# One core, a hybrid encoder layer: the side work of an attention block issued between the two score maps of the next block

## The chip, the cores and the metric

The kernel runs on one core of a Trainium2 chip. The metric is the device time of one execution in microseconds (us). The profile names the engines PE (TensorE, matmuls and transposes), PEld (its weight loads, which overlap), DVE (VectorE), ACT (ScalarE), POOL (GpSimd) and SP (SyncE, which issues nearly all DMAs of this kernel, in order); a suffix q stands for an engine's queue of such issues.

## The reference: what is computed

A layer of 1024 positions by 1024 channels in float32: a modulated RMS norm, one input projection, and two groups of four heads each on its result. Group A is a gated linear attention in both directions, computed in 16 chunks of 64 positions (GLA). Group B is a differential attention: two softmax maps for each head, the second subtracted with a factor. Their outputs go side by side through one output projection and are added to the input; a gated MLP with a convolution of width 3 and a last RMS norm follow.

```python
# GLA, one direction: S_t = diag(a_t) S_(t-1) + k_t v_t^T
chunk_update = jnp.einsum('bhnsd,bhnsv->nbhdv', k_st, v)
def step(S, inp):
    upd, dec = inp
    return dec[..., None] * S + upd, S
_, S_prev = lax.scan(step, S0, (chunk_update, chunk_decay))
o_inter = jnp.einsum('bhncd,nbhdv->bhncv', q_in, S_prev)
...
# differential attention, one block of 128 queries
s = jnp.einsum('bhiqd,bhikd->bhiqk', q_blk, k).astype(jnp.float32) * scale
s = s + bias.transpose(0, 3, 1, 2)[:, :, None]
p = jax.nn.softmax(s, axis=-1)
a = p[:, :, 0] - lam * p[:, :, 1]
return jnp.einsum('bhqk,bhkv->bhqv', a, v.astype(jnp.float32))
...
mixed = jnp.concatenate([o_a, o_b], axis=-1) @ w_out[i]
x = x + g_a[:, None, :] * mixed
```

## The kernel before, in words

The program runs through the projection, the attention, the up-projection and the down-projection in this order, with pieces of the next stage drawn into the one before. Up to the projection the instructions stand as written; from the attention on, a scheduler orders each engine's instructions at build time, from a model of when operands are ready, with the order of the program as priority. So a step that is issued earlier in the program moves ahead on every engine on which it stands, though not by a fixed number of rows.

The differential attention runs over 32 blocks of 128 queries: for each half of the positions, heads 0 to 3, four blocks each (`seq`, blocks 0 to 3 of all heads, then 4 to 7). `att_seq` (L1261) goes over them as a software pipeline whose rows are a string of steps, and the digit behind a letter is how many blocks ahead that step works:

```python
for i in range(-3, len(seq) + 3):
    for what, rest in todo:
        at = i + int(rest.rstrip("ab") or 0)
```

- `l` is `att_load` (L827): the queries of two blocks (L832) and the bias of one (L702), all on SP.
- `pa` and `pb` are `att_probs` for the first and the second map: scores on PE (`s`, L842), bias and row minimum on DVE (`p`, `mx`, L845), the exponential on ACT (L850).
- `m` is `att_mix` on DVE: L856, L858, and L860, which joins both maps into one.
- `t` is `att_T`: eight transposes on PE (`aT_ps`, L869), half copied by ACT (L871) and half by DVE (`aT`, L873).
- `o` is `att_out`: eight matmuls on PE (`o`, L888), the scaling on DVE (`on`, L889), and for the last block of a head and half the norm (ACT L895 to L897, POOL L898), whose result the next block transposes (L907) and stores (L921, L922).
- `s` is `side` (L1362), the work that goes along with block `at`. In some blocks it loads the keys of the next head (`load_k`, L817). In the first 16 blocks it takes steps of the GLA heads, in the order that the entry `glas` gives, from 1 to 3 steps a block; in the second 16 it takes steps of the output projection of the first half of the positions (L1288 on: loads L1313 and L1301, matmuls L565 to L567, the sum L1325, the transposes L380).

The GLA steps are four kinds for each head:

```python
'glas': 'L0 S0 L1 C0 S1 O0 L2 C1 S2 O1 L3 C2 S3 O2 C3 O3'
```

- `L` loads its keys, values and queries (L1010 to L1012, `gk`, `gv`, `gq`).
- `S`, the state, works in two groups: four transposes of the keys on PE (`kn_ps`, L1028), their copy on ACT (`kn`, L1029), sixteen matmuls on PE (`u_ps_0`, `u_ps_1`, L1034), copies on ACT into the state (`gs`, L1039, L1041).
- `C`, the scan, is 14 steps on DVE, each on the result of the one before (`gs`, L1049), then four DMAs on SP that rearrange the state (L1055, L1056).
- `O`, the output, works on two halves: masked scores (`pf` and `pb` on PE, L1071 and L1074; both masks on DVE, L1075 and L1076, into one buffer `att` of which there is one in all), the product (`go`, L1082 and L1085), its copy and square on ACT (L1088, `gsq` L1090), the mean on PE (`ms`, L1095), two activations on ACT (L1096, L1097), a product on DVE (L1098), one on POOL (L1099), the split into a high and a low part (ACT cast L370 `ohi`, POOL L371) and two stores on SP (L1103, L1104).

`mm` PSUM banks (two) serve `kn_ps`, `u_ps`, `pf`, `pb`, `go` and `ms`; two `ao` banks serve the transposes and `o`; two banks of double size serve the scores `s`.

Of the kernel before, what the change touches and what calls it, by code (L numbers as in the profile page):

```python
# [76 lines left out]

@with_exitstack
def hymba_kernel(ctx, tc, ins, bounds, out):
    KN = {'seq': 'X2 X3 X0 X1 Z0123 A2 A3 A0 G1 U0 C0 b0av W0v R0 g0 X4 Q1:8 W1v Q1 C1 b1av g1 N0 X5 X6 X7 Z4567 A4 A5 Q2:4 A6 G7 Q2:4 c0av Q2:4 c1av k0 Q2 C2 b2av k1 Q3:8 c2av g2 Q3 C3 b3av k2 c3av T0 P0 g3 k3 M0 E0 F0', 'att': 'l2 p1a p1b m0 t0 s0 o0', 'bias': (0, 3), 'lam': (2, 3), 'behind': (1, 2), 'sy': 7, 'wos': {'qk1': 0.75, 'gr0': 0.75, 'gr1': 0.75}, 'ord': 'gqk1 vd gv qk0 qk1 gr0 gr1 qk2 qk3', 'pf': {'gqk1': 1, 'vd': 2, 'gv': 4, 'qk0': 1, 'qk1': 1, 'qk2': 1, 'gr0': 1, 'qk3': 1, 'gr1': 1}, 'gla': [1, 2, 2, 3, 3, 3, 3, 3, 3, 3, 3, 3, 3, 3, 3, 3], 'w0': 13, 'kd': 2, 'wo': [3, 2, 2, 2, 2, 2, 1, 1, 2, 4, 3, 3, 3, 2, 3, 3], 'i1': 26, 'late': 1, 'x01': (3, 4), 'h2g': 2, 'aT': 0, 'h2y': 4, 'ld': 'x2 x3 p x0 a1 x1 a0 g x4 | r A1 h x5 x6 x7 A2 A3', 'tabs': 0, 'ada': {'gqk1': 0.75, 'vd': 1, 'gv': 1, 'qk0': 1, 'qk1': 1}, 'pre': {'gv': 0.5, 'qk0': 1.25, 'gr0': 1.25, 'qk1': 1.25, 'gr1': 1.25}, 'tab': {'vd': 1, 'gv': 1}, 'early': {'qk3': 1.25}, 'glas': 'L0 S0 L1 C0 S1 O0 L2 C1 S2 O1 L3 C2 S3 O2 C3 O3', 'aq': 1}  # L80
    nc = tc.nc
    V, S, G, T = nc.vector, nc.scalar, nc.gpsimd, nc.tensor
    x = ins["x"][0]
# [221 lines left out]
    def gen_ada(items):  # L305
# [5 lines left out]
        for n, (part, jj, q) in enumerate(halves):  # L311
# [493 lines left out]
    vd = {}  # L805
    kd = {}
# [55 lines left out]
    def att_T(h, qb):  # L862
# [3 lines left out]
        for g in range(2):  # L866
            ps = mm_ps(f"aT_ps{h}_{qb}_{g}", [P, 4, P], "ao")
            for i in range(4):
                T.transpose(ps[:, i, :], a[:, psl(4 * g + i)], ident)  # L869
            if g == KN["aT"]:  # L870
                S.copy(out=aT[:, 4 * g:4 * g + 4, :], in_=ps)  # L871
# [173 lines left out]
    def gen_gla_scan(h):  # L1045
        k2, vt, q2, q3, st = gla_of[h]
        at = lambda n: st[n % 2][:, n // 2, :]
        for n in range(1, NCH - 1):
            V.scalar_tensor_tensor(out=at(n + 1), in0=at(n), scalar=dc_sc[:, h, n - 1:n], in1=at(n + 1),  # L1049
                                   op0=ALU.mult, op1=ALU.add)  # L1050
            if n % KN["sy"] == 0:
                yield
# [138 lines left out]
    g0 = {}  # L1191
# [54 lines left out]
    behind = ExitStack()  # L1246
# [41 lines left out]
    def gen_wout(th):  # L1288
# [438 lines left out]
```

## Time and profile before

| | |
|---|---|
| median of 3 runs | 1404.78 us (1397.86 to 1410.41) |
| profiled execution | 1394.14 us, its span 1392.4 us |
| mean granted PE clock in it | 0.976 |
| PE busy | 1302.4 us, 94% of the span |
| DVE busy | 978.1 us, 70% |
| ACT busy | 633.6 us, 46% |
| POOL busy | 384.7 us, 28% |
| attention with GLA work (first 16 blocks) | 353.7 to 523.5 us of the span |
| attention with the output projection | 523.5 to about 708 us |

The span is the stretch that the profiler's rows cover; 1.74 us of the execution's time lie around it. The profile follows one execution, and the three runs beside it were not profiled. Busy shares are means over stages with different limits, so the waits are read stage by stage.

### The profile page before, as it was taken

To read this page: it belongs to the slowest core of one execution; us is meant where nothing else is said; L and a number is where in the kernel's file an instruction comes from. 1 tells how busy PE (TensorE), PEld (TensorE's weight loads), DVE (VectorE), ACT (ScalarE), POOL (GpSimd) and SP (SyncE) were. 2 spreads that over 40 slices of the span, in tenths; PEclk is the share of its full clock that TensorE was granted. 3 is DMA by queue.
4 is the path that set the end of the run, shared out by engine and by line. 5 is a ranking of instruction groups with operands and counts; after the bars stand their busy time and mean duration, and the time that the engine had idled before them with its cause. 6 is when DMAs were issued, how large, how long until landed. Compare 5 with 4: busy or idle time off the path is not lost.

```text
span 1392.4 us, 17710 instructions
## 1 busy us (share of the span) xinstructions
PE 1302.4 (94%) x6244; PEld 1066.0 (77%) x6244; DVE 978.1 (70%) x1433; ACT 633.6 (46%) x1058; POOL 384.7 (28%) x284
## 2 busy tenths in 40 slices
PE   6799999899988889998987999999999999999897
PEld 5577777678877768877865887878888888888676
DVE  3632458683676656668587979888888768977985
ACT  4542334373566635355153534444444445643354
POOL 1010011200002211003055544445444440005960
PEclk9899999999999989999997999999999999999999
DMA  8716577999976777978612423234444344975313
GB/s 269 219 59 235 178 225 231 292 339 360 336 217 184 221 224 234 268 253 246 210 63 68 130 86 107 83 111 129 129 129 121 114 146 165 385 252 186 125 65 121
DMA packets 197872, 261.56 MB, mean 188 GB/s; under 512 B 13914, under 2 KB 122711, under 8 KB 197783
## 3 DMA queue, kind: packets, MB, share of 16 engines
q1 hardware_dynamic: 197411, 260.40, 58.7%
q8 instruction: 49, 0.80, 0.2%
q14 instruction: 40, 0.33, 0.1%
q10 hardware_dynamic: 372, 0.04, 0.0%
HBM read 187.51 MB, written 68.68 MB: 184 GB/s over the span
## 4 chain that ended last, share of the span: by engine, by line
PE 68%; DVE 11%; DMA 9%; ACT 4%; issue 3%; SPq 2%; POOL 1%; ACTq 0%; DVEq 0%; POOLq 0%
PE st_up_b L565 4%; PE st_up_b L566 4%; PE st_up_b L567 4%; PE dp L566 4%; PE dp L567 4%; PE dp L565 4%; PE s L842 3%; PE st_up_c L566 3%; PE st_up_c L567 3%; PE st_up_c L565 2%; PE st_up_a L565 2%; PE st_up_a L567 2%; PE st_up_a L566 2%; PE o L888 2%; DMA q<-q_d 2%
## 5 line engine op out<-in xcount | busy, mean ns | idle before, releaser
L371 POOL TENSOR_TENSOR wlo_up<-raw_up,whi_up 128x512 fp32r<-128x512 f32 x132 | 177.0, 1348 | 213.4 <-ACT whi_up L370 200.2
L370 ACT CAST whi_up<-raw_up 128x512 fp32r<-128x512 f32 x132 | 80.6, 618 | 107.5 <-PE st_up_b L566 62.0
L566 PE MATMUL dp<-wlo_dp,dp_hi 128*128 128x512 f32 x308 | 121.8, 395 | 4.6 <-DVE wlo_dp L371 4.6
L565 PE MATMUL dp<-whi_dp,dp_hi 128*128 128x512 f32 x308 | 120.4, 393 | 3.6 <-DVE dacc L1562 3.6
L567 PE MATMUL dp<-whi_dp,db_p 128*128 128x512 f32 x308 | 119.9, 394 | 0.0
L565 PE MATMUL st_up_b<-t_hi,whi_up 128*128 128x512 f32 x264 | 104.1, 395 | 5.5 <-ACT t_hi L390 3.0
L566 PE MATMUL st_up_b<-t_lo,whi_up 128*128 128x512 f32 x264 | 103.9, 394 | 4.4 <-DVE t_lo L394 4.4
L567 PE MATMUL st_up_b<-t_hi,wlo_up 128*128 128x512 f32 x264 | 103.4, 392 | 0.0
L850 ACT ACTIVATE p<-p,mx 128x1024 f32<-128x1024 f32 x64 | 73.5, 1149 | 62.3 <-DVE mx L845 61.9
L845 DVE CUSTOM_DVE_ANT_0 p<-s,bias 128x1024 f32<-128x1024 f32 x64 | 76.7, 1218 | 29.5 <-PE s L842 16.0
L842 PE MATMUL s<-k,q 128*128 128x512 f32 x256 | 74.6, 419 | 11.4 <-DMA k<-k_d 6.8
L1432 ACT ACTIVATE cv<-u,cw 128x1024 f32<-128x1024 f32 x44 | 53.2, 1210 | 66.5 <-DVE u L433 66.4
L888 PE MATMUL o<-vd,aT 128*128 128x128 f32 x512 | 69.4, 283 | 6.9 <-ACT aT L871 3.9
L888 PEld LDWEIGHTS o<-vd,aT 128*128 128x128 f32 x512 | 65.4, 196 | 12.6 <-ACT aT L871 5.3
L371 DVE TENSOR_TENSOR wlo_dp<-da_p,whi_dp 128x512 fp32r<-128x512 f32 x77 | 67.5, 892 | 8.7 <-ACT whi_dp L370 8.5
L566 PEld LDWEIGHTS dp<-wlo_dp,dp_hi 128*128 128x128 f32 x308 | 58.5, 190 | 18.9 <-DVE wlo_dp L371 6.7
L371 DVE TENSOR_TENSOR db_p<-db_p,dp_hi 128x1024 fp32r<-128x1024 f32 (+1 forms) x42 | 59.6, 1424 | 17.4 <-ACT dp_hi L370 17.4
L565 PEld LDWEIGHTS dp<-whi_dp,dp_hi 128*128 128x128 f32 x308 | 58.7, 191 | 16.5 <-DVE dacc L1562 4.0
L565 PE MATMUL st_up_a<-b_hi,whi_up 128*128 128x512 f32 x176 | 69.1, 392 | 2.3 <-DVE b L384 1.3
L566 PE MATMUL st_up_a<-b_lo,whi_up 128*128 128x512 f32 x176 | 68.5, 389 | 0.0
L370 ACT CAST whi_dp<-da_p 128x512 fp32r<-128x512 f32 x77 | 46.4, 620 | 47.1 <-PE dp L567 35.0
L567 PEld LDWEIGHTS dp<-whi_dp,db_p 128*128 128x128 f32 x308 | 58.6, 190 | 12.0
(550 smaller groups left out, 3408.0 us busy)
## 6 DMA issues: line engine op xcount, KB each, us to landing
raw_up<-in_w_up_dram SPq DMA_DIRECT2D x88, 256.0 KB
db_p<-g_d SPq DMA_DIRECT2D x35, 512.0 KB
bias<-sk SPq DMA_DIRECT2D x32, 512.0 KB
da_p<-in_w_down_dram SPq DMA_DIRECT2D x30, 512.0 KB
raw_wada<-in_w_ada_dram SPq DMA_DIRECT2D x24, 512.0 KB
g_d<-u SPq DMA_DIRECT2D x22, 512.0 KB
g_d<-gt SPq DMA_DIRECT2D x33, 256.0 KB
x<-in_x_dram SPq DMA_DIRECT2D x16, 512.0 KB
```

The costliest lines, as they stand in the source:

```text
L370: S.copy(out=dst_hi, in_=src)
L371: lo_eng.tensor_tensor(out=dst_lo, in0=src, in1=dst_hi.bitcast(F32), op=ALU.subtract)
L565: T.matmul(ps, wh, rh, start=first, stop=False, skip_group_check=more)
L566: T.matmul(ps, wh, rl, start=False, stop=False, skip_group_check=more)
L567: T.matmul(ps, wl, rh, start=False, stop=last, skip_group_check=more)
L842: T.matmul(s[:, tsl(n)], q4[:, 2 * m + sw, :], kd[h][m][:, tsl(n)], start=(sw == 0), stop=(sw == 1))
L845: V.tensor_tensor_reduce(out=t, in0=s, in1=bias, scale=1.0, scalar=3.0e38, op0=ALU.add, op1=ALU.min, accum_out=mx)
L850: S.activation(t, t, AF.Exp, scale=-1.0, bias=mx, accum_out=z[:, m:m + 1])
L888: T.matmul(o_ps, aT[:, k, :], vd[h // 2][k // 4][:, k % 4, psl(h % 2)], start=(k == 0), stop=(k == KT - 1))
L1432: S.activation(t, u[b], AF.Identity, scale=cw[:, 44 + ci:45 + ci], bias=cw[:, 132 + ci:133 + ci])
```

## The change

One entry of the table of numbers that the kernel keeps at L80 is changed. In the loop of `att_seq` above, the row of steps was: load two blocks ahead, both maps of the next block, mix and transposes of this block, side work, output. After the change the side work of this block comes right behind the first map of the next block, ahead of its second map, the mix and the transposes. The steps themselves, their number and all other entries are the same, and so is the number of instructions on every engine.

```diff
 KN = {
...
-    'att': 'l2 p1a p1b m0 t0 s0 o0',
+    'att': 'l2 p1a s0 p1b m0 t0 o0',
...
     'kd': 2,
     'gla': [1, 2, 2, 3, 3, 3, 3, 3, 3, 3, 3, 3, 3, 3, 3, 3],
...
```

How the scheduler's order follows is shown at three places. In the names of the rows the digit or digits behind a name count the block or the half, the map and the group, and the last number is the buffer's.

**PE, the state of GLA head 2**, which goes along with the last blocks of attention head 1 (`o_3` is block 3 of head 1, `s_1_1` the second map of block 1 of head 2, `ms_1` the norm of the GLA head before). Before:

```order
L1095 MATMUL ms_1_4669<-gsq_1_4667,inv_dv 128x512
L1028 MATMUL kn_ps_0_4821<-ident,gk_4680 128x128 x4
L842 MATMUL s_1_1_4911<-k_1_4741,q_0_4696 128x512 x4
L888 MATMUL o_3_4876<-vd_0_4027,aT_3_4802 128x128 x4
L888 MATMUL o_3_4876<-vd_1_4028,aT_3_4802 128x128 x4
L869 MATMUL aT_ps_0_0_4926<-ident,p_0_0_4783 128x128 x4
L869 MATMUL aT_ps_0_1_4932<-ident,p_0_0_4783 128x128 x4
L1034 MATMUL u_ps_0_0_4827<-gv_4681,kn_0_4820 128x128 x4
L1034 MATMUL u_ps_0_1_4834<-gv_4681,kn_0_4820 128x128 x4
L1028 MATMUL kn_ps_1_4842<-ident,gk_4680 128x128 x4
L1034 MATMUL u_ps_1_0_4848<-gv_4681,kn_1_4841 128x128 x4
```

And after:

```order
L1095 MATMUL ms_1_4642<-gsq_1_4640,inv_dv 128x512
L1028 MATMUL kn_ps_0_4794<-ident,gk_4653 128x128 x4
L869 MATMUL aT_ps_3_1_4870<-ident,p_3_0_4708 128x128 x4
L1034 MATMUL u_ps_0_0_4800<-gv_4654,kn_0_4793 128x128 x4
L1034 MATMUL u_ps_0_1_4807<-gv_4654,kn_0_4793 128x128 x4
L1028 MATMUL kn_ps_1_4815<-ident,gk_4653 128x128 x4
L842 MATMUL s_1_1_4968<-k_1_4714,q_0_4696 128x512 x4
L888 MATMUL o_3_4876<-vd_0_4027,aT_3_4863 128x128 x4
L888 MATMUL o_3_4876<-vd_1_4028,aT_3_4863 128x128 x4
L1034 MATMUL u_ps_1_0_4821<-gv_4654,kn_1_4814 128x128 x4
```

The score map, `o_3` and the transposes of the next block stood between the first `kn_ps` and its `u_ps`; now four transposes stand there, and the map and `o_3` stand between the second `kn_ps` and its `u_ps`. At the state of GLA head 3 the same happens: `u_ps_0` stands directly behind `kn_ps_0`, where eight transposes and two maps stood between them, and `o_2` of head 2 and two maps come behind the second `kn_ps`. On ACT the cast `ohi_1` and then the copy `kn_0` follow the two activations behind `ms_1` in both orders, at both heads.

**DVE, the end of head 3's early blocks** (`pf`, `pb` and `go` with a half's number are of the GLA outputs of heads 2 and 3, `p_3` the maps of block 3, `gs` the scan of GLA head 3). Before, from the last scan step on:

```order
L1049 SCALAR_TENSOR_TENSOR gs_5155<-gs_5154,dc_sc,gs_5155 128x128
L1098 SCALAR_TENSOR_TENSOR go_0_5277<-go_0_5277,cols_2082,gsq_0_5279 128x512
L889 TENSOR_SCALAR on_0_5394<-o_1_5500,rz_1_5439 128x128
L1075 COPY_PREDICATED att_2096<-mf,pf_0_5562 128x512
L1098 SCALAR_TENSOR_TENSOR go_1_5379<-go_1_5379,cols_2082,gsq_1_5381 128x512
L845 ISA p_3_0_5522,mx_3_0_5523<-s_3_0_5517,bias_3_5417 128x1024
L845 ISA mx_3_0_5523 128x1
L845 ISA p_3_1_5532,mx_3_1_5533<-s_3_1_5527,bias_3_5417 128x1024
L845 ISA mx_3_1_5533 128x1
L873 COPY aT_2_5541<-aT_ps_2_1_5548 128x512
L1076 COPY_PREDICATED att_2096<-mb,pb_0_5563 128x512
```

And after, first at the last scan step:

```order
L1049 SCALAR_TENSOR_TENSOR gs_5128<-gs_5127,dc_sc,gs_5128 128x128
L1076 COPY_PREDICATED att_2096<-mb,pb_1_5317 128x512
L889 TENSOR_SCALAR on_0_5394<-o_0_5396,rz_0_5377 128x128
L1098 SCALAR_TENSOR_TENSOR go_0_5250<-go_0_5250,cols_2082,gsq_0_5252 128x512
L918 SCALAR_TENSOR_TENSOR dlo_0_5412<-oT_ps_0_5406,dw_1557,dhi_0_5411 128x512
L845 ISA p_2_1_5478,mx_2_1_5479<-s_2_1_5473,bias_2_5304 128x1024
L845 ISA mx_2_1_5479 128x1
L873 COPY aT_1_5487<-aT_ps_1_1_5494 128x512
L856 RECIPROCAL rz_2_5597<-z_2_5427 128x2
L858 SCALAR_TENSOR_TENSOR rb_2_5596<-z_2_5427,nlam,rz_2_5597 128x1
L860 SCALAR_TENSOR_TENSOR p_2_0_5424<-p_2_1_5478,rb_2_5596,p_2_0_5424 128x1024
```

and then directly behind these:

```order
L889 TENSOR_SCALAR on_0_5394<-o_1_5500,rz_1_5483 128x128
L845 ISA p_3_0_5522,mx_3_0_5523<-s_3_0_5517,bias_3_5417 128x1024
L845 ISA mx_3_0_5523 128x1
L1075 COPY_PREDICATED att_2096<-mf,pf_0_5535 128x512
L1098 SCALAR_TENSOR_TENSOR go_1_5352<-go_1_5352,cols_2082,gsq_1_5354 128x512
L1076 COPY_PREDICATED att_2096<-mb,pb_0_5536 128x512
L845 ISA p_3_1_5592,mx_3_1_5593<-s_3_1_5587,bias_3_5417 128x1024
L845 ISA mx_3_1_5593 128x1
L873 COPY aT_2_5601<-aT_ps_2_1_5608 128x512
```

Before, the last scan step came behind the second map `p_2_1`, the mix of block 2 and the mask of `pb_1`; now it is ahead of all three. The first map `p_3_0` stood behind the mask of `pf_0` and is now ahead of it, and both masks are ahead of the second map and of the copy `aT_2`.

**PE, the same place a little later**, where the scores of head 0's late blocks begin (`s_4_0` is the first map of block 4). Before:

```order
L1071 MATMUL pf_1_5591<-gq_5070,gk_5068 128x128 x4
L842 MATMUL s_4_0_5626<-k_0_5554,q_4_5510 128x512 x4
L869 MATMUL aT_ps_3_0_5651<-ident,p_3_0_5522 128x128
L842 MATMUL s_4_1_5636<-k_1_5555,q_4_5510 128x512 x4
L869 MATMUL aT_ps_3_0_5651<-ident,p_3_0_5522 128x128 x3
L869 MATMUL aT_ps_3_1_5657<-ident,p_3_0_5522 128x128 x2
```

And after:

```order
L1071 MATMUL pf_1_5564<-gq_5043,gk_5041 128x128 x4
L888 MATMUL o_2_5614<-vd_1_4151,aT_2_5601 128x128 x4
L869 MATMUL aT_ps_3_0_5679<-ident,p_3_0_5522 128x128 x4
L1074 MATMUL pb_1_5565<-gq_5043,gk_5041 128x128 x4
L842 MATMUL s_4_0_5626<-k_0_5527,q_4_5510 128x512 x4
L1095 MATMUL ms_0_5576<-gsq_0_5562,inv_dv 128x512
L842 MATMUL s_4_1_5664<-k_1_5528,q_4_5510 128x512 x4
```

The second half of `o_2` (before, it stood ahead of the product `go_0`), four transposes and `pb_1` now come between `pf_1` and the first map.

On SP, the loads of a GLA head (L1010 to L1012) now stand ahead of the attention's stores L921 and L922, where they stood behind or between them; the store L1103 of a GLA output stood ahead of the keys of head 3 and now stands behind them; and at the end of head 3's blocks the four state DMAs (L1055, L1056) stand ahead of L921 and L922, which now come between these and the loads of the next queries (L832) and keys (L817).

More of the change, by code (lines that the diff above doesn't have):

```diff
@@ L79, in hymba_kernel @@
 def hymba_kernel(ctx, tc, ins, bounds, out):
-    KN = {'seq': 'X2 X3 X0 X1 Z0123 A2 A3 A0 G1 U0 C0 b0av W0v R0 g0 X4 Q1:8 W1v Q1 C1 b1av g1 N0 X5 X6 X7 Z4567 A4 A5 Q2:4 A6 G7 Q2:4 c0av Q2:4 c1av k0 Q2 C2 b2av k1 Q3:8 c2av g2 Q3 C3 b3av k2 c3av T0 P0 g3 k3 M0 E0 F0', 'att': 'l2 p1a p1b m0 t0 s0 o0', 'bias': (0, 3), 'lam': (2, 3), 'behind': (1, 2), 'sy': 7, 'wos': {'qk1': 0.75, 'gr0': 0.75, 'gr1': 0.75}, 'ord': 'gqk1 vd gv qk0 qk1 gr0 gr1 qk2 qk3', 'pf': {'gqk1': 1, 'vd': 2, 'gv': 4, 'qk0': 1, 'qk1': 1, 'qk2': 1, 'gr0': 1, 'qk3': 1, 'gr1': 1}, 'gla': [1, 2, 2, 3, 3, 3, 3, 3, 3, 3, 3, 3, 3, 3, 3, 3], 'w0': 13, 'kd': 2, 'wo': [3, 2, 2, 2, 2, 2, 1, 1, 2, 4, 3, 3, 3, 2, 3, 3], 'i1': 26, 'late': 1, 'x01': (3, 4), 'h2g': 2, 'aT': 0, 'h2y': 4, 'ld': 'x2 x3 p x0 a1 x1 a0 g x4 | r A1 h x5 x6 x7 A2 A3', 'tabs': 0, 'ada': {'gqk1': 0.75, 'vd': 1, 'gv': 1, 'qk0': 1, 'qk1': 1}, 'pre': {'gv': 0.5, 'qk0': 1.25, 'gr0': 1.25, 'qk1': 1.25, 'gr1': 1.25}, 'tab': {'vd': 1, 'gv': 1}, 'early': {'qk3': 1.25}, 'glas': 'L0 S0 L1 C0 S1 O0 L2 C1 S2 O1 L3 C2 S3 O2 C3 O3', 'aq': 1}
+    KN = {'seq': 'X2 X3 X0 X1 Z0123 A2 A3 A0 G1 U0 C0 b0av W0v R0 g0 X4 Q1:8 W1v Q1 C1 b1av g1 N0 X5 X6 X7 Z4567 A4 A5 Q2:4 A6 G7 Q2:4 c0av Q2:4 c1av k0 Q2 C2 b2av k1 Q3:8 c2av g2 Q3 C3 b3av k2 c3av T0 P0 g3 k3 M0 E0 F0', 'att': 'l2 p1a s0 p1b m0 t0 o0', 'bias': (0, 3), 'lam': (2, 3), 'behind': (1, 2), 'sy': 7, 'wos': {'qk1': 0.75, 'gr0': 0.75, 'gr1': 0.75}, 'ord': 'gqk1 vd gv qk0 qk1 gr0 gr1 qk2 qk3', 'pf': {'gqk1': 1, 'vd': 2, 'gv': 4, 'qk0': 1, 'qk1': 1, 'qk2': 1, 'gr0': 1, 'qk3': 1, 'gr1': 1}, 'gla': [1, 2, 2, 3, 3, 3, 3, 3, 3, 3, 3, 3, 3, 3, 3, 3], 'w0': 13, 'kd': 2, 'wo': [3, 2, 2, 2, 2, 2, 1, 1, 2, 4, 3, 3, 3, 2, 3, 3], 'i1': 26, 'late': 1, 'x01': (3, 4), 'h2g': 2, 'aT': 0, 'h2y': 4, 'ld': 'x2 x3 p x0 a1 x1 a0 g x4 | r A1 h x5 x6 x7 A2 A3', 'tabs': 0, 'ada': {'gqk1': 0.75, 'vd': 1, 'gv': 1, 'qk0': 1, 'qk1': 1}, 'pre': {'gv': 0.5, 'qk0': 1.25, 'gr0': 1.25, 'qk1': 1.25, 'gr1': 1.25}, 'tab': {'vd': 1, 'gv': 1}, 'early': {'qk3': 1.25}, 'glas': 'L0 S0 L1 C0 S1 O0 L2 C1 S2 O1 L3 C2 S3 O2 C3 O3', 'aq': 1}
     nc = tc.nc
```

## The prediction

> **What bounds the kernel now.** The first line of the page gives the engines' shares.
>
> ```profile
> PE 1302.4 (94%) x6244; PEld 1066.0 (77%) x6244; DVE 978.1 (70%) x1433; ACT 633.6 (46%) x1058; POOL 384.7 (28%) x284
> ```
>
> TensorE (PE) is the bound over the whole span, so an edit that adds and removes no instruction can gain only what PE idles, and what it loses at a reduced clock, inside the stretch that the edit touches. That stretch is the attention. I cut it at the first block of the second sixteen (head 0, blocks 4 to 7) with the view by stretches; behind the bounds and the length stand the busy time of PE, PEld, DVE, ACT and POOL, then the granted PE clock, the DMA share and GB/s.
>
> ```profile
> 353.73:523.50 169.77, 151.05 (x1008) 129.11 (x1006) 112.45 (x230) 97.85 (x195) 25.44 (x21) 0.94 0.79 232
> 523.50:707.90 184.40, 175.31 (x994) 147.81 (x994) 123.72 (x207) 78.25 (x170) 25.78 (x21) 1.00 0.75 230
> ```
>
> In the first row PE idles 169.77 - 151.05 = 18.7 us and its clock is at 0.94; in the second it idles 9.1 us at full clock. The first sixteen blocks, which carry the GLA work, hold most of what can move. The list of PE's waits in that stretch (total, times, longest) says what ends the 18.7 us:
>
> ```profile
> PE s L842 <- DMA k<-k_d: 4.7, 3, 3.5
> PE u_ps L1034 <- ACT kn L1029: 2.9, 4, 1.3
> PE s L842 <- issue: 2.4, 2, 1.4
> PE o L888 <- DVE aT L873: 2.4, 1, 2.4
> PE s L842 <- DMA q<-q_d: 1.8, 2, 1.2
> PE kn_ps L1028 <- ACT gs L1041: 1.8, 3, 0.6
> ```
>
> No wait is longer than 3.5 us, and they belong to few places: the state stage of each GLA head (`u_ps`, `kn_ps`), and the change from head 3's early blocks to head 0's late ones (keys, `aT`). I read each in the timeline.
>
> **The change part by part.** No instruction is added or dropped; every term is a wait or a half-rate stretch.
>
> *End of head 3's blocks (E).* Timeline rows are start, duration, engine, line, operation, count, and in brackets the idle time before with what ended it. PE, then DVE, then SP's queue:
>
> ```profile
> 502.02 1.13 PE L1095 MATMUL ms<-gsq,inv_dv 128*128 128x512 f32 x2 [0.89 <-ACT gsq L1090]
> ...
> 508.58 1.47 PE L888 MATMUL o<-vd,aT 128*128 128x128 f32 x8 [2.36 <-DVE aT L873]
> ...
> 513.92 1.16 PE L1071 MATMUL pf<-gq,gk 64*128 64x128 f32 x8
> 518.57 2.04 PE L842 MATMUL s<-k,q 128*128 128x512 f32 x4 [3.50 <-DMA k<-k_d]
> ```
>
> ```profile
> 488.83 1.28 DVE L860 SCALAR_TENSOR_TENSOR p<-p,rb,p 128x1024 f32<-128x1024 f32 x1
> ...
> 494.81 0.73 DVE L1076 COPY_PREDICATED att<-mb,pb 128x512 f32<-128x512 int32 x1
> 495.44 1.11 DVE L1049 SCALAR_TENSOR_TENSOR gs<-gs,dc_sc,gs 128x128 f32<-128x128 f32 x3
> ...
> 504.26 0.73 DVE L1075 COPY_PREDICATED att<-mf,pf 128x512 f32<-128x512 int32 x1 [6.00 <-PE pf L1071]
> 504.89 0.74 DVE L1098 SCALAR_TENSOR_TENSOR go<-go,cols,gsq 128x512 f32<-128x512 f32 x1
> 505.54 1.23 DVE L845 CUSTOM_DVE_ANT_0 p<-s,bias 128x1024 f32<-128x1024 f32 x1
> ```
>
> ```profile
> 496.23 0.50 SPq L1055 DMA_DIRECT2D go<-gs  x1
> ...
> 508.67 4.04 SPq L817 DMA_DIRECT2D k<-k_d  x4
> ```
>
> DVE stands 6.00 us at the mask of `pf_0` while both maps of block 3 and the copy `aT_2` queue behind it; that copy is the 2.36 us that PE loses at `o_2`. After the change one map goes ahead of the mask, and on PE the second half of `o_2` goes behind `go_0` and `pf_1`, which cover the copy: -2.36. The wait for `ms` (0.89) gets transposes, a score map and `o_1` ahead of it: -0.89.
>
> The keys are what is late next. SP issues them at the end of a run that begins with the state stores L1055, and these wait for the last scan step on DVE. After the change the last step stands ahead of the mix of block 2 (1.28), its second map (1.23) and the mask of `pb_1` (0.73), so it ends about 3.2 us earlier; two stores (L921, L922) now stand inside SP's run, at 0.50 like the row of L1055, +1.0. The keys land 2.2 us earlier, so the maps could begin at 518.57 - 2.2 = 516.4. PE came to them at 513.92 + 1.16 = 515.08; without 3.25 us of waits, and with `pb_1` (1.16 like `pf`, same shape) and four transposes (0.6, half of the eight at 429.46 below) now ahead, it comes at 513.6. The wait is 2.8 instead of 3.50: -0.7. Idle time of E: -0.89 - 2.36 - 0.7 = -3.95. Bounds: 0 if every wait is only renamed, -6.75 if the keys too are in time.
>
> The clock belongs to this place as well:
>
> ```profile
> 434.00:441.00 7.00, 5.94 (x29) 5.32 (x29) 0.21 (x2) 6.34 (x12) 0.00 (x0) 0.51 0.95 302
> 508.60:513.00 4.40, 4.40 (x25) 4.40 (x26) 2.51 (x5) 1.50 (x4) 1.28 (x1) 0.61 1.07 310
> 516.00:523.00 7.00, 4.37 (x11) 3.03 (x12) 1.26 (x3) 1.08 (x2) 0.00 (x0) 0.51 1.03 314
> ```
>
> Behind the 2.36 the clock is 0.61 over 4.40 busy us, 4.40 x 0.39 = 1.7 lost; behind the 3.50 it is 0.51 over 4.37, 2.1 lost. I credit the first whole and, since a wait of 2.8 remains, half of the second: -1.7 - 1.1 = -2.8 (bounds 0 and -3.8). **E: -6.8.**
>
> *State stage of head 2 (C) and of head 3 (D)*, a timeline of each:
>
> ```profile
> 429.46 1.26 PE L869 MATMUL aT_ps<-ident,p 128*128 128x128 f32 x8
> 432.06 1.71 PE L1034 MATMUL u_ps<-gv,kn 64*128 64x128 f32 x16 [1.34 <-ACT kn L1029]
> 434.37 1.11 PE L1028 MATMUL kn_ps<-ident,gk 128*128 128x128 f32 x4 [0.60 <-ACT gs L1041]
> 436.17 3.10 PE L1034 MATMUL u_ps<-gv,kn 64*128 64x128 f32 x16 [0.69 <-ACT kn L1029]
> ```
>
> ```profile
> 461.24 2.05 PE L888 MATMUL o<-vd,aT 128*128 128x128 f32 x16 [1.04 <-ACT aT L871]
> 463.13 1.02 PE L1095 MATMUL ms<-gsq,inv_dv 128*128 128x512 f32 x2
> 463.99 0.60 PE L1028 MATMUL kn_ps<-ident,gk 128*128 128x128 f32 x4
> 464.35 1.17 PE L842 MATMUL s<-k,q 128*128 128x512 f32 x4
> 465.35 1.04 PE L869 MATMUL aT_ps<-ident,p 128*128 128x128 f32 x8
> 467.19 1.17 PE L842 MATMUL s<-k,q 128*128 128x512 f32 x4 [0.80 <-DMA k<-k_d]
> 469.08 1.71 PE L1034 MATMUL u_ps<-gv,kn 64*128 64x128 f32 x16 [0.73 <-ACT kn L1029]
> ```
>
> `u_ps` waits for ACT's copy `kn`, and this copy stands on ACT behind the whole norm of the GLA head before: `ms` on PE, two activations, DVE L1098, POOL L1099, ACT's cast L370, then the copy. In D `ms` has left PE at 463.99 and `u_ps` begins at 469.08: a chain of 5.1 us. PE fills it now with the score maps, the transposes and, in C, the `o` of block 3. The change takes most of this filling away, since the side work is issued ahead of it. In C `kn_ps` (0.4 from start to start, as 463.99 to 464.35) and four transposes (0.6) remain between `ms` and `u_ps`: a wait of 5.1 - 1.0 = 4.1. Gone are 1.34, and 0.69, since a score map and `o_3` come between the second `kn_ps` and its `u_ps`; the 0.60 stays. **C: +4.1 - 2.0 = +2.1.** In D only `kn_ps` remains between them: a wait of 5.1 - 0.4 = 4.7. Gone are 0.73, the wait for keys (0.80; the store L1103 that held SP back no longer stands ahead of those loads) and the 1.04, as `o_2` moves behind: **D: +4.7 - 2.6 = +2.1.** Bounds of both: the chain hidden by work that PE draws from elsewhere, -2.0 and -2.6, and the whole chain uncovered, 5.1 each, so +3.1 and +2.5. C's half-rate stretch (434.00 to 441.00 above) stays; I add none.
>
> Here a rule of the Trainium skill can be weighed. The rows first: both `u_ps` groups in C hold sixteen matmuls of one shape, and the second took 3.10 against 1.71, in the stretch at 0.51, with no idle time ahead of it longer than 1.34. "TensorE: Matmul & The Clock Gate", Part 1, says that the clock falls to half after an idle window of about 3.4 us and is restored after as long a busy one, the windows free-running. The half rate agrees with it; that 1.34 us of waiting was enough does not. By the page's threshold the new waits would each bring a half-rate stretch, and the sum would be that of the clock rival below; by the rows it is the sum that I take.
>
> *State stage of head 1 (A).* The second `kn_ps` had one of the three waits for `gs` in the list (0.6); after the change its `u_ps` copies are long done by then: **-0.6**, bounds 0 and -1.8 (with a wait for queries of 1.2, which also hang on scans that come earlier).
>
> *Blocks 4 to 7 of all heads* carry the output projection as side work. The 9.1 us of idle time there include a change of stage that the order doesn't shorten. I take 0; bounds +2 and -2, a fifth of those 9.1.
>
> Sum: -6.8 + 2.1 + 2.1 - 0.6 = -3.2 us against the profiled execution's 1394.14, so 1390.9. It lies 10.6 below the median of the three runs shown (1397.86 to 1410.41), and on that median, 1404.78, the forecast is **1401.6**. Up- and down-projection behind have the same instructions on a bound PE, so what the attention gains or loses comes through.
>
> **The rivals.**
>
> *The clock.* The two new waits each bring a stretch like that at 516.00, 2.1 us lost: +4.2, so +1.0 in all, 1405.8. For it: every half-rate row above lies behind a wait. Against it: the stretch of C is in the time already, and the second `u_ps` waits vanish.
>
> *SP's order, the slower one.* The GLA loads and the state stores now stand on SP ahead of stores and loads of the attention. SP is one queue; a store that waits for a scan holds all behind it. If that makes the keys late at the changes to heads 2 and 3 as they are at E now, each costs 3.50 of wait and 2.1 of clock: 2 x 5.6 = +11.2, total +8.0, **1412.8**. It decides once the scans' stores wait longer than the 6 us between the issue at 508.67 + 4.04 and a map that needs them. For it: the 3.50, longest of the list. Against it: the scans run earlier, and in D the keys get out from behind a store.
>
> *The new waits are filled.* ACT reaches the `kn` copy early enough in C and D, and E loses all its waits: -2.0 - 2.6 - 6.75 - 3.8 - 1.8 = -17.0, **1387.8**. For it: side work issued early gives each chain more time until its result is needed. Against it: the order on ACT still has the cast L370 ahead of the copy, and on PE `u_ps` directly behind.
>
> *That the change does nothing* is out: the rows in the order have moved at each of these places.
>
> **How the numbers follow.** Forecast 0.50, the clock 0.17, SP 0.17, filled 0.16. The forecast's own bounds add up to -19 and +7.6 us, but only if all terms fall to one side. The range goes from the filled case to SP's, 1387 to 1413; half of each of these two, 0.16 together, lies outside. One per cent, 14 us, is about what a measurement of this kernel can tell from no change. Faster by more than that needs 1390.7 or less: the filled case, and the low end of the forecast in exchange for its slower half, 0.15. Slower by more needs 1418.8, SP's case with a third late key: 0.07. The remaining 0.78 is no change that can be told.
>
> **What would show it.** E right: no wait of 6 us on DVE at the `pf_0` mask, no wait for `aT` of 2 us on PE, the keys' wait at the first late block 2 to 3 us, and a stretch at full clock ahead of it. C and D right: two waits `u_ps <- kn` above 4 us, the longest in PE's list, where the longest was 1.3. A right: two waits for `gs` instead of three. Clock rival: stretches near 0.5 behind these two waits, and a granted clock of the first sixteen blocks at or below 0.94. SP's: waits for keys or biases of 3 us and more at heads 2 and 3. I would be wrong altogether if the time moved in blocks 4 to 7 or behind the attention, where I have put nothing.

## The result, and the profile after

The changed kernel took 1387.05 us (median of 4 runs, 1385.39 to 1390.9) against 1407.4 for the kernel before (4 runs, 1397.86 to 1410.41): a ratio of 0.9902, interval 0.9873 to 0.9932. Run once more beside the experiments it took 1384.99 against 1401.93, ratio 0.9890 (0.9863 to 0.9917). It is faster by about 1%, 15 to 20 us, where 3.2 were forecast. 1387.05 lies at the very edge of the range of 1387 to 1413, 14.6 us below the point forecast of 1401.6, and the second time of 1384.99 lies outside it: that the first one falls inside is luck. Single executions far above all others of their kernel, one of 1642.8 us at a granted clock of 0.75 among them, are left out of what follows.

The profiled executions differ by less: 1388.06 us against 1394.14, spans 1386.4 and 1392.4. The first line of the page after, and the two stretches of the attention cut at the same times as before:

```profile
PE 1302.7 (94%) x6244; PEld 1069.5 (77%) x6244; DVE 978.6 (71%) x1433; ACT 634.5 (46%) x1058; POOL 389.0 (28%) x284
```

```profile
353.73:523.50 169.77, 157.31 (x1051) 136.78 (x1049) 118.73 (x234) 100.07 (x199) 25.30 (x22) 0.93 0.78 236
523.50:707.90 184.40, 175.49 (x976) 147.16 (x975) 123.82 (x205) 80.15 (x176) 29.33 (x23) 0.99 0.76 236
```

The engines' work is the same. In the first stretch PE is busy for 157.31 us instead of 151.05, so 6.3 us of idle time are gone (12.5 are left of 18.7); in the second the idle time stays at 8.9 of 9.1. The clock is what it was (0.93 and 0.94). All of PE's waits in the first stretch, after:

```profile
PE u_ps L1034 <- ACT kn L1029: 8.2, 2, 4.3
PE aT_ps L869 <- DVE on L889: 2.3, 1, 2.3
PE s L842 <- DMA k<-k_d: 1.5, 1, 1.5
PE aT_ps L869 <- DVE p L860: 0.3, 1, 0.3
```

The six rows shown of before counted 15 waits; now it is 5 in all. The two long waits for `kn` are there. Of the waits that a transfer ended, 4.7 for keys and 1.8 for queries, 1.5 for keys remains; the 2.4 under "issue" have gone as well. The place E in the timelines of PE, DVE and SP after:

```profile
502.90 1.02 PE L1095 MATMUL ms<-gsq,inv_dv 128*128 128x512 f32 x2
...
513.44 1.16 PE L1074 MATMUL pb<-gq,gk 64*128 64x128 f32 x8
516.08 1.77 PE L842 MATMUL s<-k,q 128*128 128x512 f32 x4 [1.49 <-DMA k<-k_d]
```

```profile
493.07 1.11 DVE L1049 SCALAR_TENSOR_TENSOR gs<-gs,dc_sc,gs 128x128 f32<-128x128 f32 x3
...
505.05 0.75 DVE L1075 COPY_PREDICATED att<-mf,pf 128x512 f32<-128x512 int32 x1
```

```profile
493.87 0.51 SPq L1055 DMA_DIRECT2D go<-gs  x1
...
508.29 3.02 SPq L817 DMA_DIRECT2D k<-k_d  x4
```

Neither `ms` nor the mask of `pf_0` has idle time in front of it, where 0.89 and 6.00 us stood, and the wait for `aT` is gone. The places C and D:

```profile
426.12 0.60 PE L1028 MATMUL kn_ps<-ident,gk 128*128 128x128 f32 x4
426.56 0.60 PE L869 MATMUL aT_ps<-ident,p 128*128 128x128 f32 x4
431.00 3.06 PE L1034 MATMUL u_ps<-gv,kn 64*128 64x128 f32 x16 [3.83 <-ACT kn L1029]
...
463.62 0.60 PE L1028 MATMUL kn_ps<-ident,gk 128*128 128x128 f32 x4
468.54 3.06 PE L1034 MATMUL u_ps<-gv,kn 64*128 64x128 f32 x16 [4.32 <-ACT kn L1029]
```

These are chains of 4.9 us from `kn_ps` to `u_ps` (5.1 before, in D), covered by one group of transposes or by nothing.

To compare several executions I took marks from PE's timeline: the first score map, the first `kn_ps` of GLA heads 2 and 3, the norm `ms` at the end of head 2's output (502.02 and 502.90 above), the last `ms`, and the first row of the up-projection. All are durations in us, worked out from starts; the third profile of before and the second of after come from the experiments.

| profile | its time | first score at | to `kn_ps` 2 (A) | to `kn_ps` 3 (C) | to `ms` (D) | to last `ms` (E) | to the up-projection | attention |
|---|---|---|---|---|---|---|---|---|
| before, 1st | 1394.1 | 353.7 | 72.6 | 37.7 | 38.0 | 33.6 | 172.6 | 354.5 |
| before, 2nd | 1395.9 | 356.0 | 71.3 | 37.7 | 38.1 | 33.2 | 176.1 | 356.4 |
| before, 3rd | 1403.2 | 359.0 | 73.1 | 37.3 | 39.6 | 33.8 | 176.2 | 360.0 |
| after, 1st | 1388.1 | 355.4 | 70.7 | 37.5 | 39.3 | 24.8 | 176.7 | 348.9 |
| after, 2nd | 1384.5 | 355.2 | 70.4 | 37.9 | 38.9 | 23.5 | 176.6 | 347.3 |

In the means the attention is 8.9 us shorter (357.0 to 348.1), and E alone is 9.4 shorter. But the marks move with the order of the program, so a stage doesn't hold the same rows in both kernels. The stages from that `ms` to the last `ms` and from there to the up-projection, before and after, in the first profiles (length, then PE's busy time and its matmuls):

```profile
502.02:535.67 33.65, 27.73 (x164) 23.44 (x165) 19.34 (x32) 15.86 (x31) 5.95 (x5) 0.85 0.85 252
535.67:708.27 172.60, 163.51 (x912) 137.32 (x911) 113.96 (x192) 70.44 (x155) 22.38 (x19) 1.00 0.77 236
```

```profile
502.90:527.68 24.78, 23.29 (x154) 19.52 (x153) 16.85 (x28) 12.78 (x25) 5.58 (x4) 0.93 1.03 329
527.68:704.34 176.66, 167.99 (x933) 140.76 (x931) 118.25 (x198) 74.29 (x164) 23.80 (x19) 0.99 0.76 230
```

E holds ten matmuls fewer after the change, and the last stage twenty more. What can be compared is PE's idle time, the length less the busy time:

| PE's idle time | A | C | D | E | late blocks | attention |
|---|---|---|---|---|---|---|
| before, 1st | 5.2 | 3.7 | 3.9 | 5.9 | 9.1 | 27.8 |
| before, 2nd | 4.1 | 3.7 | 4.1 | 6.1 | 11.3 | 29.3 |
| before, 3rd | 5.9 | 5.5 | 5.5 | 4.2 | 11.3 | 32.3 |
| after, 1st | 2.6 | 4.0 | 4.5 | 1.5 | 8.7 | 21.1 |
| after, 2nd | 2.3 | 4.5 | 4.5 | 1.6 | 7.9 | 20.7 |

PE's busy time over the whole attention is 327.2 us in both means, so the 8.9 us are idle time: in the means 3.9 from E, 2.7 from A and 2.3 from the late blocks.

### The profile page after: what moved, and what is told of

Same layout as the page of the kernel before. It is cut to its first block, busy times and chain, and to the rows that moved or that the text cites. A ratio compares the mean times of both kernels' runs of the same rounds, so it can differ in the third digit from the quotient of the medians.

```text
span 1386.4 us, 17727 instructions
## 1 busy us (share of the span) xinstructions
PE 1302.7 (94%) x6244; PEld 1069.5 (77%) x6244; DVE 978.6 (71%) x1433; ACT 634.5 (46%) x1058; POOL 389.0 (28%) x284
## 4 chain that ended last, share of the span: by engine, by line
PE 69%; DVE 12%; DMA 5%; issue 4%; ACT 3%; POOL 3%; SPq 2%; ACTq 0%; DVEq 0%; POOLq 0%
PE st_up_b L565 4%; PE st_up_b L566 4%; PE st_up_b L567 4%; PE s L842 3%; PE dp L566 3%; PE dp L565 3%; PE dp L567 3%; PE o L888 3%; PE st_up_c L566 3%; PE st_up_c L567 3%; PE st_up_c L565 3%; PE st_up_a L566 2%; PE st_up_a L565 2%; PE st_up_a L567 2%; PE wo_ps L567 2%
## 5 line engine op out<-in xcount | busy, mean ns | idle before, releaser
L845 DVE CUSTOM_DVE_ANT_0 p<-s,bias 128x1024 f32<-128x1024 f32 x64 | 77.3, 1217 | 14.9 <-PE s L842 12.9
L842 PE MATMUL s<-k,q 128*128 128x512 f32 x256 | 78.0, 427 | 2.4 <-DMA k<-k_d 1.5
L370 ACT CAST whi_dp<-da_p 128x512 fp32r<-128x512 f32 x77 | 46.4, 620 | 49.5 <-PE dp L567 37.5
```

The source lines that it names most:

```text
L370: S.copy(out=dst_hi, in_=src)
L842: T.matmul(s[:, tsl(n)], q4[:, 2 * m + sw, :], kd[h][m][:, tsl(n)], start=(sw == 0), stop=(sw == 1))
L845: V.tensor_tensor_reduce(out=t, in0=s, in1=bias, scale=1.0, scalar=3.0e38, op0=ALU.add, op1=ALU.min, accum_out=mx)
```

## The experiments

**The kernel before, twice more.** No edit; the question is the scatter of the kernel before.

> The kernel before once more, unchanged, for a second profile. Of its runs so far the profiled one took 1394.1 us and the others 1397.9 to 1410.4, while the changed kernel's four runs lie within 1385.4 to 1390.9, so between the profiled executions 6 us are gained and between the medians 20. Theory 1 (the step at the end of head 3's early blocks, E, is also where the kernel before scatters, since keys that come late there are late by a varying time): a profile with more than 1400 us shows the keys' wait at the first late block longer than 3.5 us, by most of the difference to 1394.1. Rival (the scatter is elsewhere: start, projection, change to the up-projection): that wait stays at 3.5 +- 0.5 and the difference lies outside 353 to 530 us. Time 1398 to 1411.

It came out at 1398.16 against 1402.44 for the same program in the runs beside it, ratio 0.9966 (0.9938 to 0.9994). So differences of 0.3% are not read below. Its profile, 1395.9, was too quick to settle the question.

> The kernel before, a third profile. Its runs scatter from 1390 to 1412 us, those of the changed kernel from 1382 to 1391; the two profiles so far took 1394.1 and 1395.9. Theory 1 (the scatter is in waits that a DMA ends, in the blocks from the first late one on): an execution of 1400 us or more has its additional time in waits for keys, queries or oT between 500 and 600 us of the span. Rival (it lies ahead of the attention or in the projections): these waits sum up to the same 7 to 9 us as in the first two profiles.

This execution took 1403.2. Two things are in it. First, it comes to the attention at 359.0, 5.3 us later than the first profile, although it is the same program. One of PE's waits ahead of the attention, in the first and the third profile of before and in the changed kernel:

```profile
PE pr_gr L565 <- DVE gr L765: 1.7, 1, 1.7
```

```profile
PE pr_gr L565 <- DVE gr L765: 5.3, 1, 5.3
```

```profile
PE pr_gr L565 <- DVE gr L765: 2.6, 1, 2.6
```

This wait in the projection, 1.7 and 5.3 in the same program, accounts for 3.6 of the 5.3 us. Second, the attention takes 360.0 against 354.5, with 4.9 us of DMA-ended waits behind the last `ms` (2.4 in the first profile; keys 2.62 and 1.07, `oT` 1.20); of the 5.5, 1.6 lie in D's stage and 3.6 behind the last `ms`, and the keys' wait at E was even shorter (1.74). So the place that I blamed, E's keys, is not where this kernel scatters, and neither theory holds alone: 5.3 us lie ahead of the attention and 5.5 in it, and 1.6 are won back behind it.

**The changed kernel once more.**

> The changed kernel once more, beside the other kernels of this study. Expected 1385 to 1391 against 1400 to 1404 for the kernel before, ratio 0.989 to 0.993, with the waits of its first profile: u_ps <- kn 3.8 and 4.3 us, keys at the first late block 1.5 us.

1384.99, ratio 0.9890, as said above, and all three waits within 0.1 us of the first profile: 3.83 and 4.33 for `kn`, 1.53 for keys. Its six runs lie within 6 us.

**The first or the second sixteen blocks alone.** In `att_seq`, S is the early place and s the late one:

```diff
-    'att': 'l2 p1a p1b m0 t0 s0 o0',
+    'att': 'l2 p1a S0 p1b m0 t0 s0 o0',
...
-                else:
+                elif (what == "S") == (at in range(16)):
                     side(at)
```

> The side work ahead of the second map in the first sixteen blocks only (GLA work); in the second sixteen it stays where it was before. Theory 1: the gain is made in the GLA blocks, so nearly all of it is here: 1387 +- 4, E as in the changed kernel (keys' wait 1 to 3 us, no wait for aT of 2 us), two waits u_ps <- kn of about 4 us. Rival (the output projection's blocks carry the gain): 1400 or more, with the same waits in the first sixteen.

1393.39 us, ratio 0.9921 (0.9892 to 0.9949): most of the gain, though the time is above theory 1's 1383 to 1391. E takes 27.0 us, with 155 matmuls as in the changed kernel (24.8 and 23.5 there), and the keys' wait is 2.52.

With `range(16, 32)` in that place:

> The side work ahead of the second map in the second sixteen blocks only (output projection); the GLA blocks are as before. Theory 1: within 4 us of the kernel before, 1400 to 1410, with the waits 1.34 at u_ps, 2.36 for aT and 3.5 for keys still there. Rival (the output projection's blocks carry the gain): 1390 or less, and the stretch from the first late block to the up-projection shorter by 5 us or more.

1409.85, ratio 1.0052 (1.0026 to 1.0078): alone the second half is a loss, though not far above the 0.3% by which the same program differed. The time is in theory 1's range, but the keys' wait is not 3.5. Its timeline at the first late block and one head later:

```profile
521.31 2.04 PE L842 MATMUL s<-k,q 128*128 128x512 f32 x4 [6.24 <-DMA k<-k_d]
```

```profile
563.43 1.20 PE L842 MATMUL s<-k,q 128*128 128x512 f32 x4 [1.46 <-DMA k<-k_d]
566.96 1.62 PE L842 MATMUL s<-k,q 128*128 128x512 f32 x3 [2.33 <-DMA k<-k_d]
```

The keys' wait grows from 3.50 to 6.24 and more such waits follow: in the whole attention PE waits 14.9 us for transfers, against 9.0, 12.2 and 11.2 in the three profiles of before, and 1.5 in both of after. Keys that come late are the sign of my slower rival, but its mechanism isn't shown: SP's run from the first state store to the keys is 12.3 us long, as before (12.4). Counted from the first score map, the keys are issued 0.5 us later than in the first profile of before and are there 1.8 later, while PE comes to them 1.0 earlier. The waits of SP in front of the keys' issues, before and here:

```profile
SPq L817 <- DMA x<-in_x_dram: 2.4, 2, 1.7
```

```profile
SPq L817 <- DMA x<-in_x_dram: 3.0, 2, 2.4
```

So SP stands among the keys' issues until loads of `x` (L1301), which it issued ahead of them, have landed; through which resource, the profile doesn't say.

**Blocks 7 and 11 put back.** `at in set(range(32)) - {7, 11}` in the same place; they carry the state of GLA heads 2 and 3.

> The changed kernel with the side work of blocks 7 and 11 alone put back to where it was before; these two blocks carry the state stages of GLA heads 2 and 3. Theory (the two waits u_ps <- kn of 3.8 and 4.3 us, and the half-rate stretch behind each, are what the change pays there): the two waits fall to below 1.5 us each, and the time to 1380 to 1384, 3 to 7 us below the changed kernel. Rival (these waits cover work that then comes later, so their end frees nothing): the waits go and the time stays at 1387 +- 2.

The ratio was 0.9951 (0.9931 to 0.9970), so some 7 us slower than the changed kernel and not faster. The rows below are from a second run of this kernel.

> The changed kernel with the side work of blocks 7 and 11 put back, again, because its first profile came from a disturbed execution; its runs then had a median of 1396.6 us. Theory 1 (waits u_ps <- kn are a net cost of the change): 1380 to 1384. Theory 2 (what the early state work costs in waits it gives back later, since the scan, the output and the DMAs that hang on it come earlier): the two waits are below 1.5 us, yet the time is 1390 to 1398, and the stretch behind the scans of heads 2 and 3 or the keys' wait at the first late block is longer than in the changed kernel by as much.

1396.75, ratio 0.9964 (0.9939 to 0.9989), beside 0.9890 for the changed kernel in the same job. The rows of head 2's state, of head 3's, and of the first late block:

```profile
435.47 1.71 PE L1034 MATMUL u_ps<-gv,kn 64*128 64x128 f32 x16 [1.10 <-ACT kn L1029]
439.61 2.98 PE L1034 MATMUL u_ps<-gv,kn 64*128 64x128 f32 x16 [1.15 <-ACT kn L1029]
```

```profile
471.25 3.09 PE L1034 MATMUL u_ps<-gv,kn 64*128 64x128 f32 x16 [4.33 <-ACT kn L1029]
```

```profile
521.93 2.04 PE L842 MATMUL s<-k,q 128*128 128x512 f32 x4 [2.60 <-DMA k<-k_d]
```

Only head 2's wait went (head 3's order stayed as in the changed kernel), and its stage took 37.7 us, as ever: the 3.83 became 1.10, 1.15 and two small ones. What is lost comes behind it: the attention takes 354.3 us instead of 348.1, D's stage 40.5 instead of 39.1, and waits for transfers are 4.9 instead of 1.5. (E's 27.6 hold 165 matmuls, so they can't be set beside the 24.2.) That fits theory 2 for head 2: the early state work pays for its wait. It isn't shown by itself, since by the steps that each block takes the edit also puts back the state DMAs of head 1 (block 7) and the first scores of head 2's output (block 11).

**Blocks 12 to 15, and 12 to the end.** `range(12, 16)`:

> The side work ahead of the second map in blocks 12 to 15 only, those of attention head 3 early half, behind which the keys of the first late block are waited for. The scan of GLA head 3 (blocks 9 to 13) is only in part moved. Theory 1 (the gain is made at this place, E, by the DVE order and by scans that end earlier): 1392 to 1396, no wait for aT of 2 us, keys' wait shorter than 3.5 us. Rival (the gain needs the whole chain of GLA steps to come earlier): 1398 to 1402, with the keys' wait at 3 us or more.

1392.70, ratio 0.9947 (0.9925 to 0.9968). E takes 25.7, the wait for `aT` is gone, and the keys' wait is 2.4:

```profile
517.51 1.17 PE L842 MATMUL s<-k,q 128*128 128x512 f32 x4 [2.40 <-DMA k<-k_d]
```

Four blocks bring half of the gain, most of it at E. The text above has the scan of head 3 in the wrong blocks. A load takes one step, a state two, a scan three and an output five, and the blocks take 1, 2, 2 and then 3 steps; that puts head 3's state in block 11 and its scan in blocks 13 and 14, so all of the scan moves here. The rows agree: counted from the first score map, the first state store L1055 comes at 138.4 us, as in the changed kernel (138.4), against 142.5 before. The next text repeats the mistake in its theory 2. With `range(12, 32)`:

> The side work ahead of the second map from block 12 on, to the end; blocks 0 to 11 as before, so the two waits u_ps <- kn of about 4 us are not there. Alone, blocks 12 to 15 had a ratio of 0.9947 to the kernel before, the second sixteen blocks 1.0052, the first sixteen 0.9921 and all of them 0.9890. Theory 1 (early work in the second sixteen is harmful only where the keys of the first late block are late, and with the scan of head 3 early in blocks 12 to 15 it is harmless): 0.986 to 0.993, 1381 to 1392, keys' wait below 2.5 us and no wait for keys or queries of 1 us or more behind 540 us. Theory 2 (the scan of head 3, which begins in block 10, has to come early as a whole): 0.995 to 1.003, 1395 to 1405, with a keys' wait above 2.5 us or waits for keys and queries behind 540 us that sum to 3 us or more.

1393.03, ratio 0.9946 (0.9920 to 0.9971). The profile looks like the changed kernel's, with 1.73 us for keys and 0.70 behind; the runs don't show it (1386.5 to 1401.7, the profiled one 1387.8). Early side work in the second sixteen is harmless here, as theory 1 has it, but the time is between the two theories. By the ratios blocks 0 to 11 add 0.5%, though these come from two jobs; by the profiles they add nothing, since the attention takes 347.3 us here and 348.9 and 347.3 in the changed kernel. Their waits `u_ps <- kn` at least don't speak against them.

**The keys earlier.** In `side`, the keys of the first late block are loaded with block 13 instead of 14, on the kernel before:

```diff
-        if i % 4 == KN["kd"] and i + 4 - KN["kd"] < len(seq):
-            load_k(seq[i + 4 - KN["kd"]][0])
+        if i % 4 == (1 if i == 13 else KN["kd"]) and i != 14 and i + 4 - KN["kd"] < len(seq):
+            load_k(seq[i + 4 - i % 4][0])
```

> The kernel before, with one edit: the keys of the first late block are loaded with block 13 instead of 14, so on SP they stand ahead of the state DMAs. Theory 1 (the keys hang on the scan only through SP's order, and a late key costs its wait and a half-rate stretch): the keys' wait of 3.5 us is gone, the wait for aT of 2.4 us stays, and the time falls by 3 to 6 us, to 1396 to 1399. Rival (the loads themselves are slow there, since the DMA queue is full): the wait stays at 2 us or more, and the time within 2 us of the kernel before.

1395.80, ratio 0.9978 (0.9953 to 1.0003). The keys' wait at the first late block is gone and the one for `aT` stays, as theory 1 has it:

```profile
513.07 1.16 PE L888 MATMUL o<-vd,aT 128*128 128x128 f32 x8 [2.37 <-DVE aT L873]
```

E takes 26.3 with as many matmuls as before, 7 us less, yet the time falls by some 3 us and the attention by 1.2, within what this can tell. The late blocks take 179.1 us instead of 175.0, and A and C are over 1 us longer each; the waits there for the next head's keys (2.21) and `oT` (1.32) are no longer than in the profiles of before. So a wait taken away at E need not come through. The same edit on the changed kernel:

> The changed kernel with the keys of the first late block loaded with block 13 instead of 14, the edit that alone made the kernel before 3 to 6 us faster. Theory (the 1.5 us that are left of the keys' wait are SP's order): the wait is gone, no half rate there was left to win, so 1382 to 1385, 0 to 3 us below the changed kernel. Rival (the earlier keys push the state DMAs back, and the GLA output of head 3 waits for these): a wait in front of go or pf of 1 us or more, and 1386 to 1390.

1397.53, ratio 0.9976 (0.9950 to 1.0003), slower than the changed kernel. With this edit SP issues the keys at 474.1, 34 us earlier than in the changed kernel. Instead of for keys, a map waits until a store of `go` has landed (through which resource, the profile doesn't say):

```profile
508.59 0.70 PE L842 MATMUL s<-k,q 128*128 128x512 f32 x2 [1.58 <-DMA o_d<-go]
```

PE's idle time in E is 2.9 us instead of 1.5 (the stage holds 163 matmuls, the changed kernel's 154 and 155), and waits for weights, queries and keys of 2.6 us in all come in the late blocks, where the changed kernel has none. The rival was right in its sign only: the time is above its range, the row is another, and the state stores are not pushed back (the first comes at 135.9 us from the first score map, 138.4 in the changed kernel). The attention is 2.8 us longer than the changed kernel's; where the rest of the loss lies isn't known.

**`kn` copied by DVE.** On the changed kernel:

```diff
-            S.copy(out=kn, in_=kps)
+            V.tensor_copy(out=kn, in_=kps)
```

> The changed kernel with one edit: the copy kn behind the transposes of the GLA keys is made by DVE instead of ACT. Theory (the waits u_ps <- kn of 3.8 and 4.3 us are the chain ms, two activations, DVE L1098, POOL, cast, copy, about 4.9 us, and bind because of ACT's order alone): the copy gets out from behind POOL and the cast, so the wait in front of head 3's u_ps falls to about 2.4 us and head 2's to below 2, the half-rate stretches behind them get shorter, and the time falls by 3 to 8 us, to 1377 to 1383. Rival (as with blocks 7 and 11: what is won at these waits is paid later): the waits fall and the time stays at 1385 +- 2.

1404.39, ratio 1.0019 (0.9996 to 1.0041): the whole gain is lost. The rows of head 3's state, with DVE's copy, and one in the late blocks:

```profile
471.88 0.69 DVE L1029 COPY kn<-kn_ps 128x512 f32<-128x512 f32 x1 [1.47 <-DMA o_d<-ohi]
```

```profile
472.67 3.06 PE L1034 MATMUL u_ps<-gv,kn 64*128 64x128 f32 x16 [4.05 <-ACT ohi L370]
```

```profile
581.11 0.47 PE L842 MATMUL s<-k,q 128*128 128x512 f32 x1 [3.77 <-DMA q<-q_d]
```

At head 2 the scheduler put other work into the gap and the wait is gone. At head 3 it stayed at 4.05, since DVE's copy stood idle until a store of `ohi` was done (`kn` and `ohi` take buffers of one pool of five, probably the reason): ACT's order was not all that held it. And from the last `ms` to the up-projection this kernel takes 185.9 us instead of 176.6, though that stage holds ten matmuls fewer, with waits of 3.77, 0.71, 1.08 and 0.77 for queries and keys. No kernel tried was faster than the changed one.

## Why the prediction was right and wrong

**What bounds the kernel** held: PE's work is the same to 0.3 us, and the difference in the attention is idle time. 6.6 of its 8.9 us lie in the blocks with GLA work; 2.3 lie in the late blocks, where I had put nothing and had called a movement a sign of being wrong.

**E was right in mechanism and nearly in size.** Of the 9.4 us by which the stage is shorter, a part is only ten matmuls that now stand behind its end. The idle time fell by 3.9, where 3.95 were forecast. For the clock 2.8 were forecast; busy time times what the granted clock lacks to 1 gives 4.2, 2.7 and 5.9 us in the three profiles of before and 1.6 and 0 in the two of after, so by this estimate 3.5 were won. The waits of 0.89 and 2.36 and DVE's 6.00 went as worked out; with blocks 12 to 15 alone the 2.36 goes too, while 0.92 for `ms` stays.

The keys' wait was put at 2.8 and is 1.49, and the way there holds two errors that cancel. The changed kernel's profile comes to the attention 1.7 us later, so I count from the first score map. Counted so, the scan ends 4.1 us earlier (3.2 forecast), but SP's run from the first state store to the keys grew from 12.4 to 14.4 us, twice what I had added, so that the keys are issued 2.1 earlier (2.2 forecast). PE comes to them 2.2 earlier (1.5 forecast), and the keys are there 4.2 earlier, because the four issues took 3.02 us instead of 4.04 and the time from the last issue to the map fell from 5.9 to 4.8. SP's wait for loads of `x` in front of these issues, 2.4 us in the first profile of before, 1.7 and 2.2 in the others, is in neither profile of after; all that is left there, in the first of them, is this:

```profile
SPq L817 <- DMA o_d<-dlo: 0.2, 1, 0.2
SPq L817 <- DMA o_d<-ohi: 0.2, 1, 0.2
```

The prediction had no term for that wait.

**C and D: the waits were right, the net was not.** 4.1 and 4.7 us were forecast, 3.83 and 4.32 came, with the chain named. But I put the net at +2.1 each, and the stages took 37.7 against 37.6, and 39.1 against 38.6: +0.1 and +0.5 in the means; PE's idle time in them is unchanged in the means (4.3 and 4.2, 4.5 and 4.5; 0.3 to 0.8 more than in the first profile of before). This is the largest error among the terms: in D I had left 0.60, 0.30 and 0.59 standing as waits, and in C 0.60, and all of these went as well; and the two new waits are 0.65 shorter together.

**The clock rival had the right premise.** A half-rate stretch does stand behind each of the new waits:

```profile
431.00:436.00 5.00, 4.87 (x23) 4.38 (x24) 0.08 (x1) 2.89 (x6) 0.80 (x1) 0.51 0.79 249
468.50:474.00 5.50, 5.33 (x24) 4.74 (x25) 0.86 (x5) 3.34 (x7) 0.84 (x1) 0.51 0.73 237
```

But the kernel before had one at both places too, the 0.51 from 434 to 441 and this one in D, behind waits of 0.80, 0.73 and 0.60:

```profile
471.90:475.30 3.40, 3.40 (x15) 3.01 (x13) 0.00 (x0) 3.34 (x7) 0.00 (x0) 0.52 0.66 216
```

They moved and did not multiply. Of E's two, one of about 3 us behind the keys' wait is left in the first profile of after and none in the second, and A got one, behind a wait of 2.29 us for `on`:

```profile
384.00:390.00 6.00, 6.00 (x30) 5.68 (x29) 3.77 (x10) 1.03 (x3) 0.00 (x0) 0.50 0.72 177
```

The clock over the GLA blocks is 0.93 against 0.94, and since PE's busy time in the attention is the same, what the clock won at E was lost elsewhere, A's new stretch among it. Nor is such a stretch certain: in the third profile of before, C had waits of 1.34 and 1.15 and kept the full clock:

```profile
432.12:469.38 37.26, 31.81 (x238) 27.57 (x236) 24.72 (x51) 22.82 (x46) 8.11 (x7) 1.00 0.61 195
```

On the rule of the Trainium skill that was weighed ("TensorE: Matmul & The Clock Gate", Part 1, idle windows of about 3.4 us): waits of 3.83 and 4.32 do bring the half rate, as it says; one of 2.29 brought it too, and so did waits of at most 1.34.

**A and the late blocks were too small.** A was put at -0.6 and gave -1.8, with 2.7 less idle time: the waits for queries (1.24) and under "issue" (1.38) went, none for `gs` is left where I had kept two, and one of 2.29 for `on` came that I had not seen. For the late blocks I took 0. The stage is 1.7 us longer in the means (175.0 to 176.7) because it holds twenty matmuls more; its idle time is 2.3 shorter, and its waits for transfers fell from 2.4, 4.7 and 4.9 us to none.

**The size.** The terms missed by 5.7 us in the attention: -3.2 against -8.9. In idle time, C and D came out 4.3 lower than forecast, the late blocks 2.3 and A 2.1, against the 2.8 credited to the clock, of which nothing is left over the whole attention. The larger part of the distance to the medians is another step: I added the difference to the median of before as if the profiled execution were a typical one. It was a quick one. Its attention, 354.5, is 2.5 below the mean of three profiles, and its way to the attention the quickest of all. The changed kernel's ten runs lie within 1381.8 to 1390.9 and are close to its profiles, those of before reach 1410. In the spans' means the three profiles of before and the two of after differ by 11.4 us, 0.9 of them ahead of the attention and 1.6 behind it; for the rest up to the 15 to 20 of the medians there is no profile, and its place stays open.

**What carries the gain** beside E's waits are transfers. The sum of DMA-ended waits of PE over the attention went from 9.0, 12.2 and 11.2 us to 1.5 and 1.5. The listing of the first stretch and the runs with blocks 7 and 11 put back fit one account: state work that is early makes the scan, the state stores and, behind them on SP, queries and keys early. With blocks 12 to 15 alone it is shown at one place, E: the state stores come 4.1 us earlier and half of the gain is there. That this order on SP is the cause in A and at the late blocks as well is argued from the orders and not shown; each of the eight other kernels tried had 0.7 to 6.3 us of such waits behind the last `ms`, but none of them changes SP's order there and nothing else.

**The other rivals.** The time of the filled case (1387.8) came, but not its mechanism: the new waits were not filled. SP's rival did not come in this kernel; in the one with the second sixteen blocks alone the keys are later, but not by SP's run behind the state stores.

## What to carry to other kernels

A wait that a change will add is quickly found by following the chain behind it, but its price is the difference to all that waited in that stage before: add up the whole stage, small waits too, and don't leave some standing. Where an edit reorders the program, a stage between two marks can hold other rows than before: count them, and compare idle times rather than lengths. Work on which a chain of DMAs hangs can pay for being early even where PE then waits for it, and the return shows up in other rows, as waits for transfers that no longer come. One profiled execution may be a quick one: compare its time with the spread of the runs ahead of adding a difference to their median.

## What the runs showed of the hardware

The same program came to the attention between 353.7 and 359.0 us, with one wait in the projection between 1.7 and 5.3. PE's clock stood at about 0.5 for 3 to 7 us behind a few waits of 0.6 to 1.3 us close together, just as behind single ones of 2.3 and 4.3; in one profile waits of 1.34 and 1.15 left it at 1.00. SP's four issues of the keys took 4.04 us in all with waits for earlier loads among them, at 0.45 to 0.46 us each, and 3.02 us without, at 0.47 to 1.08 each.
